# A conv-FFN whose modulation steps, copies and first splits stand in other places

## The chip, the cores and the metric

The kernel runs on one core of a Trainium2 chip. The core has five engines with a queue of instructions each: TensorE (PE in the profile) multiplies matrices and writes its results to PSUM, VectorE (DVE) and ScalarE (ACT) do the element-wise work, GpSimd (POOL) helps them, and SyncE (SP) issues most of the DMA transfers. An engine works through its own queue in program order, and semaphores make one engine wait for another. The metric is the device time of one execution in microseconds (us); the median of several runs counts.

## What is computed

The reference is a transformer of two layers over 1024 rows of 1024 columns and 256 context rows. Layer 0 mixes a gated recurrence with latent attention, layer 1 is a differential attention. Behind each attention stands a conv-FFN, and every normalization is modulated: its shift and scale (and the gates of the branches) are rows of `silu(c) @ w_mod + b_mod`, with `w_mod` of 1024 x 6144 per layer.

```
def conv_ffn(u, w_up, conv_w, conv_b, w_down):
    a, g = jnp.split(u @ w_up, 2, axis=-1)
    g = dwconv(g, conv_w, conv_b, FFN_PAD)
    return (jax.nn.gelu(g) * a) @ w_down
```

`a` and `g` have 2816 columns each, and the convolution runs over three neighbouring rows of the sequence. All is in float32.

## The kernel before

**Products.** A float32 product is made as three TensorE passes (`mm3`, L116 to L118): high times high, high times low, low times high. So each operand is split ahead (`split`): ScalarE casts the high part (L283) and VectorE subtracts it for the low part (L98).

**Up projection** (`up_sequence`). It runs over 22 tiles f of 128 columns of `a` and of `g`. The two halves of the sequence and the two halves of the inner dimension make a 2 x 2 block product, which is done with seven block products in place of eight, by sums of the blocks of the weight (`up_sums`, L997 to L1000) and of the normalized rows (the operands "11", "t1", "t2", "t3", "21", "t4", "22"). Each block product is 12 matmuls of 128x512 into one PSUM bank. Bank B takes four of them in turn: `p1`, then t2 (in `p6`), t3 and t4. Between them its content is copied away by ScalarE: to `p` (`p1_out`, L1062), to the sum `a` and to `g` (both in `take`, L1037). `a`, `g` and `p` have one buffer each. For the tile ahead VectorE convolves `g` (L930 to L932), ScalarE makes the gelu (L933), VectorE multiplies with `a` (L1118), and the result goes to DRAM as `hid`. The body of the loop over f therefore finishes tile f - 1 while it computes tile f. In layer 0 the 256 context rows add two smaller products per tile (`ctx_product`, PSUM tile pC) and an own convolution. The first product of the first tiles may be done in the stage ahead (`self.p1`, L984); in layer 1 these are tiles 0 and 1. The queues hold the instructions in the order in which the code issues them (`manual_schedule`).

**Modulation.** While TensorE works, VectorE makes the products with `w_mod` in chunks of 512 columns (`mod_chunk_dve`): a chunk is a generator of six steps. The first zeroes the accumulator `macc` and loads a 128x1024 piece of `w_mod` into a buffer `mr`, of which there is one; each of the next four accumulates the piece (L194, four instructions for two columns `c` and `c_ctx`, two for one) and loads the next; the last sums over partitions with 4 or 8 small matmuls or two wide ones on TensorE (L204 or L211, PSUM tile `modps`) and copies the result away (L206). `some_mods()` runs one step. Before, each tile of layer 0 has such a place twice behind t1 and once behind `second` (the copy of t3's result), and layer 1 has one each. Nine chunks stand in the up projection of layer 0, three in the down projection of layer 0 and two in the up projection of layer 1.

**Down projection** (`ffn_down`). For rounds of three or four row tiles it runs over the 22 blocks f; each needs a piece of `w_down` and of `hid` (`hr`), loaded and split. **Output projection** (`out_proj`), ahead of the FFN: for each row tile it multiplies, adds the residual, normalizes (`scaled`: a Square on ScalarE at L257 which writes into `xn`, and a product with the row's scale at L260), and turns the rows with transposes on TensorE (`turned`, L270, PSUM tile `ntp`). **Front of layer 1** (`layer1_front`): a list of stages per row tile, each with a lag in steps, set by `staggered`; `scale` makes the row's scale (`rs_t`), `norm` transposes.

Of the kernel before, what the change touches and what calls it, by code (L numbers as in the profile page):

```python
# [18 lines left out]
P = 128  # L19
# [40 lines left out]
class K:  # L60
# [728 lines left out]
    def out_proj(self, l, w_name, tiles, get_yT, begin, units=()):  # L789

        nc, io = self.nc, self.io
        with ExitStack() as st:
            Y = self.sb(st, f"outy{l}", side="right")
            O = self.sb(st, f"out{l}")
            nw = NW - l
            where = [None] * nw + [O] * (KT - nw)
            us = list(units) + [self.unit(io[w_name][k * P:(k + 1) * P, :], pool=where[k], bufs=max(1, where.count(where[k])) if where[k] else 4)
                                for k in range(len(units), KT)]
            gas = {}
            y, h = {}, {}  # L800

            def load(t):
                y[t] = get_yT(Y, t)

            def product(t):
                xt = O.tile([P, D], F32, tag="x", bufs=2, name="x")
                nc.sync.dma_start(xt, (self.h0 if l == 0 else self.h1)(t))
                ps = self.PS.tile([P, 2, 512], F32, tag="p2", bufs=4, name="ops")
                for k in range(KT):
                    for a, n, j in TURNS[t == tiles[0]]:  # L810
                        if k == a and isinstance(y.get(t + n), tuple):
                            made = y[t + n][j]()
                            if j:
                                y[t + n] = made
                    for b in range(2):
                        self.mm3(ps[:, b, :], y[t][k], [x[:, b * 512:(b + 1) * 512] for x in us[k]], k == 0, k == KT - 1)
                h[t] = O.tile([P, D], F32, tag="tmp", bufs=3, name="tmp")
                c = int(t >= NTX)
                if c not in gas:
                    gas[c] = self.ga(O, l, 0, c, "ga")  # L820
                nc.vector.tensor_mul(h[t], ps.rearrange("p a b -> p (a b)"), gas[c])
                (nc.vector if t == tiles[-1] else nc.gpsimd).tensor_tensor(h[t], h[t], xt, op=ADD)
                nc.sync.dma_start(self.hm_d[t], h[t])

            def fill(t):
                if t == tiles[-1]:
                    begin()

            def norm(t):

                xn = O.tile([P, D], F32, tag="xn", bufs=1, name="xn")
                junk = xn.rearrange("p (k c) -> p k c", c=P)
                self.scaled(O, h[t], xn, junk, eng=nc.vector if t == tiles[-1] else None)
                c = slice(t % 4 * P, (t % 4 + 1) * P)
                if t < NTX:
                    self.turned(xn, self.AB2[0], lambda k: self.V[f"{k // 4 + 1}{t // 4 + 1}"][:, k % 4, c])
                    self.column_sums(t)
                else:
                    v = O.tile([P, KT, P], F32, tag="tmp", bufs=3, name="v")
                    self.turned(xn, self.AB2[1], v)  # L840
                    self.split(v, *(x[:, :, (t - NTX) * P:(t - NTX + 1) * P] for x in self.uc))

            self.staggered(tiles, (load, 0), (product, 1 + l), (fill, LAG_N + l), (norm, LAG_N + l))
# [75 lines left out]
    def split_new(self, x, pool=None, tag="w", bufs=4):  # L919

        n = x.shape[-1]
        hi, lo = ((pool or self.W).tile([P, n], F32R, tag=tag + y, bufs=bufs, name="w" + y) for y in "hl")
        self.split(x, hi, lo)
        return hi, lo

# [20 lines left out]
    def ctx_gate(self, F, f, pg):  # L946
        nc = self.nc
        nc.scalar.copy(self.cg[:, 1:1 + CTX], pg)
        gc = F.tile([P, CTX], F32, tag="cgc", bufs=2, name="gc")
        self.convolved(0, f, self.cg, gc, CTX)  # L950
        return gc

# [62 lines left out]
    def up_sequence(self, l, st, F0, chunks):  # L1015
# [25 lines left out]
        def some_mods():  # L1041
            if mods:
                mods.pop(0)()
# [29 lines left out]

        X = banks(0)
        p1(X)
        p1_out(X)
        self.split_columns(U, "t2")
        p6(X)
        self.split_columns(U, "t1")
        product(X["E"], X["s"], 0, "t1", True)  # L1080
# [20 lines left out]
        raws = self.fetch_up(l, 2)  # L1101
        F = self.sb(st, f"later{l}")
        mods += [x for ch in chunks for x in self.mod_steps(F, *ch)]
        per = -(-len(mods) // (NF - 2))
        for f in range(1, NF + 1):
            Y = step.pop(f - 1)
            if f < NF:
# [2 lines left out]
            take(g[:, 1:513], Y["B"], Y["p1"])  # L1110
            gc = F.tile([P, SEQ], F32, tag="gc", name="gc")
            if f < NF:
                X["s"] = self.split_13(X["raw"])
                p1_out(X)
            self.convolved(l, f - 1, g, gc, SEQ)
            product(Y["E"], Y["s4"], 0, "22", False)
            nc.vector.tensor_add(Y["sum"][:, h2], Y["sum"][:, h2], Y["E"])
# [6 lines left out]
            if here:  # L1124
                X["c"] = bank("C")
                self.ctx_product(X["c"][:, :CTX], [X["a21"], [y[:, h2] for y in X["g"]]])
            p6(X)
            product(X["E"], X["s"], 0, "t1", True)
            some_mods()
            if per > 2:  # L1130
                some_mods()
            if here:
                cgc = self.ctx_gate(F, f, X["c"][:, :CTX])
            if f + 1 < NF:
# [13 lines left out]
            if f + 1 < NF:  # L1148
                N["g"] = self.split_new(raws[1])
            product(X["B"], X["g"], 512, "t4", False)  # L1150
            if f + 2 < NF:
                raws = self.fetch_up(l, f + 2)
        while mods:
            some_mods()

    def mod_steps(self, pool, l, ch, nctx):

# [3 lines left out]
    def ffn_down(self, l, rounds, dst, chunks, after):  # L1161

        nc, io = self.nc, self.io
        with ExitStack() as st:
            F = self.sb(st, f"down{l}")
            gas = [self.ga(F, l, 1, c, f"ga{c}") for c in range(2 if l == 0 else 1)]
            extra = []
            if after:
                Un = self.sb(after, "u1cols", side="right")
# [26 lines left out]
                        lambda: self.turned(xn, AB, v), lambda: self.split(v, *u)]  # L1196

            with self.tc.manual_schedule():
                for i in range(3):
                    fetch(i)  # L1200
                split(0)
                for r, tiles in enumerate(rounds):
                    with ExitStack() as s2:
                        PS = self.PS = self.ps(s2, f"psD{l}{r}")
# [5 lines left out]
                        for f in range(NF):  # L1210
                            i = r * NF + f
                            if i + 3 < len(items):
                                fetch(i + 3)
                            if f == 8:
                                for t in tiles:
                                    hts[t] = F.tile([P, D], F32, tag="ht", bufs=8, name="ht")
# [27 lines left out]
    def layer1_front(self):  # L1244

        nc, io = self.nc, self.io
        with ExitStack() as st:
# [4 lines left out]
            with ExitStack() as st2:  # L1252
# [91 lines left out]
                        self.load1(0, "q")  # L1344
                        self.load1(0, "k")
                early = (lambda f: lambda item: f(item[1] + n0) if item[0] == 4 and item[1] + n0 < NT else None)
                self.staggered(items, (early(load), 0), (early(scale), 4), (early(norm), 7), (project, 4), (finish, 5), (first_head, 8))

    def lam_prep(self):

# [219 lines left out]
    def build(self, stop=99):  # L1570
        nc, tc, io = self.nc, self.tc, self.io
        with ExitStack() as st:
# [48 lines left out]
            with ExitStack() as s2:  # L1621
                F0 = self.sb(s2, "begun0")
                self.p1 = {}
                with ExitStack() as s3:
# [3 lines left out]
                    self.ctx_place(F0)  # L1628
                    self.AB2 = [self.mod_finish(0, 1, c) for c in range(2)]
                    self.out_proj(0, "w_out_ab", [*range(NTX, NT), *range(NTX)], self.yT0, lambda: self.begin0(F0))  # L1630
                self.ffn_up(0, F0, [(1, ch, 2) for ch in range(4)] + [(0, ch, 2) for ch in (10, 11)] + [(1, ch, 1) for ch in range(4, 7)])
                self.ctx_columns.close()
            columns = st.enter_context(ExitStack())
            self.ffn_down(0, [range(0, 4), range(4, 7), range(7, NT)], lambda t: self.h1_d[t], range(7, 10), columns)
            with ExitStack() as s2:
                self.PS, self.twos = self.ps(s2, "psL"), 4
                self.lam_prep()
# [70 lines left out]

# [9 lines left out]
```

## Time and profile before

| | us |
|---|---|
| runs | 3426.54, 3425.10, 3422.24 |
| median | 3425.1 |
| profiled execution | 3431.7 |
| its span in the trace | 3429.9 |
| TensorE busy | 3186.3 |
| VectorE busy | 2360.9 |
| ScalarE busy | 1412.1 |
| GpSimd busy | 945.2 |

The span is the time from the first to the last instruction of the profiled execution, which is 1.8 us shorter than its time. Times of rows count from the start of the span. The stages by their rough place: output projection of layer 0 to 877, its up projection to 1505, its down projection to 1845, front of layer 1 to 2185, attention to 2595, output projection to 2735, up projection of layer 1 to 3180, down projection to the end.

### The profile page before, as it was taken

Reading aid. Unit: us, or ns where it says so; the run is one execution under the profiler, and the core shown is the slowest. Engines: PE = TensorE matmul, PEld = TensorE weight load, DVE = VectorE, ACT = ScalarE, POOL = GpSimd, SP = SyncE. Lnnn points to the kernel's source line nnn. Section 1 sums busy time; section 2 is a strip of 40 time slices with the busy share of each in tenths; the row PEclk is TensorE's granted clock in tenths of the full one; section 3 lists DMA queues with packets and bytes.
Section 4 is the critical chain, followed back from the end, with each engine's and each line's share of the span. In section 5 each row is a group of like instructions: output and inputs, shape, how many; then the busy total and the mean of one; then the engine's idle time right before and its main releaser. Section 6 shows DMA issues by size and latency. Waiting matters only on the chain.

```text
span 3429.9 us, 43450 instructions
## 1 busy us (share of the span) xinstructions
PE 3186.3 (93%) x16262; PEld 2633.3 (77%) x16262; DVE 2360.9 (69%) x3381; ACT 1412.1 (41%) x2444; POOL 945.2 (28%) x654
## 2 busy tenths in 40 slices
PE   8998889989799999989899999888888889999998
PEld 4777778878578778868777887777777768888887
DVE  6468978855776777643566687599997687666443
ACT  3355766733422223322243222477763333333322
POOL 2223578864000000000122223277764200000010
PEclk9999999999899999999999999999999999999999
DMA  6224953344122223234755355444414122223553
GB/s 261 70 77 129 285 141 94 89 137 134 47 96 97 97 97 111 97 123 151 249 192 182 120 139 131 146 114 126 111 62 160 62 86 101 90 74 98 181 180 124
DMA packets 232298, 434.07 MB, mean 127 GB/s; under 512 B 21484, under 2 KB 147692, under 8 KB 230296
## 3 DMA queue, kind: packets, MB, share of 16 engines
q1 hardware_dynamic: 230216, 424.49, 39.3%
q10 hardware_dynamic: 1872, 6.82, 0.6%
q8 instruction: 128, 2.10, 0.2%
q14 instruction: 82, 0.67, 0.1%
HBM read 319.89 MB, written 111.34 MB: 126 GB/s over the span
## 4 chain that ended last, share of the span: by engine, by line
PE 54%; DVE 14%; DMA 3%; issue 3%; ACT 3%; POOL 1%; SPq 0%; DVEq 0%; ACTq 0%; POOLq 0%
PE acc L118 4%; PE pB L116 4%; PE pB L118 4%; PE pB L117 4%; PE acc L116 4%; PE acc L117 4%; DVE m L1456 3%; PE pj L116 3%; PE pj L117 3%; PE pj L118 3%; DVE p L1472 3%; PE pE L118 2%; PE pE L116 2%; PE pE L117 2%; PE ops L117 2%
## 5 line engine op out<-in xcount | busy, mean ns | idle before, releaser
L98 DVE TENSOR_TENSOR wl<-wr,wh 128x1024 fp32r<-128x1024 f32 (+2 forms) x285 | 348.8, 1233 | 92.9 <-ACT wh L283 63.4
L116 PE MATMUL acc<-wh,hh 128*128 128x512 f32 x792 | 312.5, 395 | 18.7 <-ACT wh L283 17.1
L118 PE MATMUL acc<-wl,hh 128*128 128x512 f32 x792 | 312.5, 395 | 9.6 <-DVE wl L98 8.9
L117 PE MATMUL acc<-wh,hl 128*128 128x512 f32 x792 | 310.6, 392 | 4.5 <-DVE hl L98 4.5
L1236 POOL TENSOR_TENSOR ht<-ht,dtmp 128x1024 f32<-128x1024 f32 x17 | 45.7, 2715 | 857.1 <-DVE dtmp L1235 857.1
L283 ACT CAST wh<-wr 128x1024 fp32r<-128x1024 f32 (+1 forms) x221 | 220.9, 1008 | 83.4 <-DVE wr L999 72.4
L98 POOL TENSOR_TENSOR wl<-wf,wh 128x1280 fp32r<-128x1280 f32 x64 | 221.9, 3468 | 106.3 <-ACT wh L1491 94.7
L1451 PE MATMUL S<-k,q 128*128 128x512 f32 (+1 forms) x768 | 197.8, 382 | 55.7 <-ACT p L1462 55.5
L116 PE MATMUL pB<-ht,wh 128*128 128x512 f32 x528 | 210.4, 398 | 16.5 <-ACT ht L283 6.5
L98 DVE TENSOR_TENSOR hl<-hr,hh 128x512 fp32r<-128x512 f32 (+1 forms) x110 | 76.0, 691 | 206.7 <-ACT hh L283 206.6
L118 PE MATMUL pB<-lt,wh 128*128 128x512 f32 x528 | 210.3, 398 | 2.2 <-DVE lt L98 2.0
L117 PE MATMUL pB<-ht,wl 128*128 128x512 f32 x528 | 209.5, 397 | 0.8 <-DVE wl L98 0.8
L194 DVE SCALAR_TENSOR_TENSOR macc<-wr,sc,macc 128x512 f32<-128x512 f32 x192 | 135.8, 748 | 105.2 <-DMA wr<-w_mod 104.1
L283 ACT CAST hh<-hr 128x512 fp32r<-128x512 f32 (+1 forms) x110 | 63.7, 579 | 325.0 <-PE acc L118 242.0
L1462 ACT ACTIVATE p<-S,m 128x1280 f32<-128x1280 f32 x128 | 170.8, 1334 | 60.6 <-DVE m L1456 57.5
L1456 DVE TENSOR_REDUCE m<-S 128x1 f32<-128x1280 f32 x128 | 187.1, 1479 | 6.2 <-PE S L1451 5.6
L116 PEld LDWEIGHTS acc<-wh,hh 128*128 128x128 f32 x792 | 149.8, 189 | 53.4 <-ACT wh L283 21.8
L177 POOL MEMSET macc<- 128x512 f32 x24 | 12.4, 526 | 636.8 <-PE modps L211 283.3
L118 PEld LDWEIGHTS acc<-wl,hh 128*128 128x128 f32 x792 | 149.7, 189 | 49.4 <-DVE wl L98 18.6
L1451 PEld LDWEIGHTS S<-k,q 128*128 128x128 f32 x768 | 124.9, 193 | 77.2 <-ACT p L1462 64.5
L116 PE MATMUL pj<-wh,u 128*128 128x512 f32 x448 | 177.6, 396 | 2.5 <-DVE qT L98 2.5
L117 PE MATMUL pj<-wh,u 128*128 128x512 f32 x448 | 178.0, 397 | 0.0
(414 smaller groups left out, 9178.3 us busy)
## 6 DMA issues: line engine op xcount, KB each, us to landing
wr<-ffn_down SPq DMA_DIRECT2D x110, 512.0 KB
wr<-ffn_up SPq DMA_DIRECT2D x90, 512.0 KB
wr<-w_mod SPq DMA_DIRECT2D x76, 512.0 KB
hid<-gc SPq DMA_DIRECT2D x44, 512.0 KB
k<-dk SPq DMA_DIRECT2D x14, 1280.0 KB
hr<-hid SPq DMA_DIRECT2D x66, 256.0 KB
wr<-w_in_c SPq DMA_DIRECT2D x24, 512.0 KB
mr<-w_mod SPq DMA_DIRECT2D x20, 512.0 KB
```

The lines of the kernel that those rows point to most:

```text
L98: e.tensor_tensor(out, x, hi.bitcast(F32), op=SUB)
L116: mm(out, a[0], b[0], start=start, stop=False, skip_group_check=onto)
L117: mm(out, a[1], b[0], start=False, stop=False, skip_group_check=onto)
L118: mm(out, a[0], b[1], start=False, stop=stop, skip_group_check=onto)
L177: nc.gpsimd.memset(acc[c], 0.0)
L194: nc.vector.scalar_tensor_tensor(acc[c], raw[:, kk * 512:(kk + 1) * 512], self.sc[:, 2 * u + kk, c:c + 1], acc[c], op0=MUL, op1=ADD)
L283: self.nc.scalar.copy(hi, x)
L1236: (nc.vector if last else nc.gpsimd).tensor_tensor(hts[t][:, c], hts[t][:, c], tmp[:, c], op=ADD)
L1451: nc.tensor.matmul(Y["S", m][:, c0:c0 + n], heads[h]["q"][m][:, t * P:(t + 1) * P], heads[h]["k"][x, m, j], start=(x == 0), stop=(x == 1))
L1456: nc.vector.tensor_reduce(Y["m", m], Y["S", m][:, :TOK], axis=AX.X, op=ALU.max, negate=True)
L1462: nc.scalar.activation(Y["p", m], Y["S", m][:, :TOK], AF.Exp, bias=Y["m", m], accum_out=Y["s"] if m else s0[:, h, t:t + 1])
L1472: nc.vector.scalar_tensor_tensor(Y["p", 0], Y["p", 1], Y["tt"], Y["p", 0], op0=MUL, op1=ADD)
```

## The change

- In the loop of the up projection the copy of `p` is issued ahead of the split of `s` (`split_13`); at its head, behind the split of t2.
- One modulation step stands in each of four places of a tile: ahead of `p6`, behind t1, behind `second`, behind t4. Three more chunks are made in the up projection of layer 0, and none in its down projection.
- `xn` in `out_proj` has two buffers.
- The first weight and the first `hid` block of the down projection are loaded and split in the last two tiles of the up projection (`fetch_down`, `self.ahead`); the gates' rows (`ga`) are loaded later in `ffn_down`.
- In the front of layer 1 `scale` has lag 5 for 4 and `norm` 8 for 7.
- `cgc` has one buffer, tiles of the splits are 1024 wide whatever is split, and the scratch of the DMA rings is 512.

```diff
             def norm(t):
-                xn = O.tile([P, D], F32, tag="xn", bufs=1, name="xn")
+                xn = O.tile([P, D], F32, tag="xn", bufs=2, name="xn")
...
-        hi, lo = ((pool or self.W).tile([P, n], F32R, tag=tag + y, bufs=bufs, name="w" + y) for y in "hl")
+        hi, lo = ((pool or self.W).tile([P, n if pool else 1024], F32R, tag=tag + y, bufs=bufs, name="w" + y)[:, :n] for y in "hl")
...
-        gc = F.tile([P, CTX], F32, tag="cgc", bufs=2, name="gc")
+        gc = F.tile([P, CTX], F32, tag="cgc", bufs=1, name="gc")
...
         p1(X)
+        self.split_columns(U, "t2")
         p1_out(X)
-        self.split_columns(U, "t2")
         p6(X)
...
-        per = -(-len(mods) // (NF - 2))
         for f in range(1, NF + 1):
...
             if f < NF:
+                p1_out(X)
                 X["s"] = self.split_13(X["raw"])
-                p1_out(X)
             self.convolved(l, f - 1, g, gc, SEQ)
...
+            some_mods()
             p6(X)
             product(X["E"], X["s"], 0, "t1", True)
             some_mods()
-            if per > 2:
-                some_mods()
...
             product(X["B"], X["g"], 512, "t4", False)
+            some_mods()
             if f + 2 < NF:
                 raws = self.fetch_up(l, f + 2)
-        while mods:
-            some_mods()
+            elif f + 2 == NF:
+                raws = self.fetch_down(l)
+            else:
+                self.ahead = self.split_new(raws[1]), self.split_new(raws[0])
...
+    def fetch_down(self, l):
+        w, x = (self.W.tile([P, 1024], F32, tag="wr", bufs=NWR, name="wr") for _ in range(2))
+        self.nc.sync.dma_start(w, self.io["ffn_down"][l, :P, :])
+        self.nc.sync.dma_start(x[:, :512], self.hid_d[0, :, :512])
+        return w, x[:, :512]
...
-                for i in range(3):
+                parts[0] = self.ahead
+                for i in range(1, 3):
                     fetch(i)
-                split(0)
...
+                            if i == 4:
+                                gas = [self.ga(F, l, 1, c, f"ga{c}") for c in range(2 if l == 0 else 1)]
...
-                self.staggered(items, (early(load), 0), (early(scale), 4), (early(norm), 7), (project, 4), (finish, 5), (first_head, 8))
+                self.staggered(items, (early(load), 0), (early(scale), 5), (early(norm), 8), (project, 4), (finish, 5), (first_head, 8))
...
-                self.ffn_up(0, F0, [(1, ch, 2) for ch in range(4)] + [(0, ch, 2) for ch in (10, 11)] + [(1, ch, 1) for ch in range(4, 7)])
+                self.ffn_up(0, F0, [(1, ch, 2) for ch in range(4)] + [(0, ch, 2) for ch in (10, 11)] + [(1, ch, 1) for ch in range(4, 10)])
...
-            self.ffn_down(0, [range(0, 4), range(4, 7), range(7, NT)], lambda t: self.h1_d[t], range(7, 10), columns)
+            self.ffn_down(0, [range(0, 4), range(4, 7), range(7, NT)], lambda t: self.h1_d[t], (), columns)
```

ScalarE in a late tile of layer 1's up projection, before (`s` is the sum of weight blocks that is split for t1 and t3, `wh` the high part; what an instruction waits for stands in brackets):

```order
L1037 COPY g<-pB 128x512 [waits PE_49]
L283 CAST wh<-s 128x1024
L1062 COPY p<-pB 128x512 [waits DVE_49,PE_49,Activation_49]
L933 ACTIVATE gc<-gc 128x1024 [waits DMAHW5_49,DVE_49]
L283 CAST wh<-s 128x512 [waits PE_49,Activation_49]
L1037 COPY a<-pB 128x512 [waits DVE_49,PE_49]
```

The same place after:

```order
L1037 COPY g<-pB 128x512 [waits PE_49]
L1062 COPY p<-pB 128x512 [waits DVE_49,PE_49]
L283 CAST wh<-s 128x1024
L933 ACTIVATE gc<-gc 128x1024 [waits DMAHW3_49,DVE_49]
L283 CAST wh<-s 128x512 [waits PE_49,Activation_49]
L1037 COPY a<-pB 128x512 [waits DVE_49,PE_49]
```

The copy of `p`, which waits for TensorE, has moved from behind the 128x1024 cast to ahead of it; the rest has kept its order.

VectorE in the up projection of layer 0, before, from the sum of weight blocks to the next tile (`modps` holds the sums of a chunk):

```order
L1000 TENSOR_TENSOR s<-wr 128x512
L1071 TENSOR_TENSOR g<-g,pE 128x512
L206 COPY mcol<-modps 128x8
L1145 TENSOR_TENSOR a<-p,pA 128x512
L954 TENSOR_TENSOR gc<-gc,pC 128x256
L98 TENSOR_TENSOR wl<-wr,wh 128x1024
L98 TENSOR_TENSOR wl<-s,wh 128x1024
```

The same engine after, in the third tile of a cycle (L1143 is L1145 of before):

```order
L1000 TENSOR_TENSOR s<-wr 128x512
L1071 TENSOR_TENSOR g<-g,pE 128x512
L194 SCALAR_TENSOR_TENSOR macc<-wr,sc,macc 128x512 x4
L1143 TENSOR_TENSOR a<-p,pA 128x512
L954 TENSOR_TENSOR gc<-gc,pC 128x256
L98 TENSOR_TENSOR wl<-wr,wh 128x1024
L206 COPY mcol<-modps 128x8
L237 SCALAR_TENSOR_TENSOR A<-mcol,cols 128x8 x2
L98 TENSOR_TENSOR wl<-s,wh 128x1024
```

The last accumulation now stands behind t3's copy, and the finish of the chunk behind t4, at the end of the tile.

SyncE between the up and the down projection of layer 0, before (`hr` is a block of `hid`):

```order
L1119 DMA hid<-gc 128x1024
L955 DMA hid<-gc 128x256
L1119 DMA hid<-gc 128x1024
L244 DMA ga<-ga_132 128x1024
L244 DMA ga<-ga_133 128x1024
L1181 DMA hr<-hid 128x512
L1178 DMA wr<-ffn_down 128x1024
```

And after:

```order
L955 DMA hid<-gc 128x256
L1161 DMA wr<-ffn_down 128x1024
L1162 DMA wr<-hid 128x512
L1186 DMA wr<-ffn_down 128x1024
L1118 DMA hid<-gc 128x1024
L955 DMA hid<-gc 128x256
L1118 DMA hid<-gc 128x1024
L1189 DMA hr<-hid 128x512
L1186 DMA wr<-ffn_down 128x1024
```

The first loads of the down projection now stand two stores of `hid` earlier, and the rows of the gates no longer stand ahead of them.

## Rows read from the trace of the kernel before

**Rows 1.** The page, part 1: busy time, share of the span, instructions.

```profile
PE 3186.3 (93%) x16262; PEld 2633.3 (77%) x16262; DVE 2360.9 (69%) x3381; ACT 1412.1 (41%) x2444; POOL 945.2 (28%) x654
```

**Rows 2.** Windows: from:to, length, busy time per engine, granted clock, DMA share, GB/s.

```profile
877.00:1505.00 628.00, 583.25 (x2938) 487.90 (x2936) 436.68 (x588) 185.91 (x277) 7.83 (x15) 0.95 0.27 91
2790.00:3170.00 380.00, 380.00 (x1656) 309.72 (x1655) 268.35 (x308) 131.88 (x176) 0.53 (x1) 1.00 0.27 91
...
2747.00:2765.00 18.00, 14.39 (x58) 10.58 (x58) 17.80 (x19) 5.16 (x6) 0.53 (x1) 1.00 0.00 0
...
1020.00:1026.00 6.00, 6.00 (x33) 6.00 (x34) 4.51 (x8) 2.36 (x4) 1.05 (x2) 0.57 0.01 3
```

**Rows 3.** Timeline of a tile of layer 1's up projection: start, duration, [idle before, releaser].

```profile
2963.66 1.05 ACT L283 CAST wh<-s 128x1024 fp32r<-128x1024 f32 x1
2965.99 0.59 ACT L1062 COPY p<-pB 128x512 f32<-128x512 f32 x1 [1.27 <-issue]
...
2971.78 0.59 ACT L1037 COPY a<-pB 128x512 f32<-128x512 f32 x1 [0.84 <-DVE gc L1118]
...
2964.74 1.23 DVE L98 TENSOR_TENSOR wl<-s,wh 128x1024 fp32r<-128x1024 f32 x1 [2.55 <-ACT wh L283]
...
2970.47 1.22 DVE L1118 TENSOR_TENSOR gc<-gc,a 128x1024 f32<-128x1024 f32 x1 [0.53 <-ACT gc L933]
...
2965.51 0.40 PE L118 MATMUL pB<-l,wh 128*128 128x512 f32 x1
...
2973.96 0.39 PE L116 MATMUL pB<-ht,wh 128*128 128x512 f32 x1
```

**Rows 4.** Waits over the whole span: total us, times, longest.

```profile
DVE macc L194 <- DMA wr<-w_mod: 104.1, 31, 6.8
```

**Rows 5.** Timeline of two tiles of layer 0's up projection, VectorE and TensorE.

```profile
1046.77 2.74 DVE L194 SCALAR_TENSOR_TENSOR macc<-wr,sc,macc 128x512 f32<-128x512 f32 x4 [4.26 <-DMA wr<-w_mod]
1049.42 0.41 DVE L930 TENSOR_SCALAR gc<-cg,cols 128x256 f32<-128x256 f32 x1
...
1057.30 2.74 DVE L194 SCALAR_TENSOR_TENSOR macc<-wr,sc,macc 128x512 f32<-128x512 f32 x4
...
1060.88 1.22 DVE L98 TENSOR_TENSOR wl<-wr,wh 128x1024 fp32r<-128x1024 f32 x1
1062.02 1.22 DVE L98 TENSOR_TENSOR wl<-s,wh 128x1024 fp32r<-128x1024 f32 x1
...
1068.87 0.68 DVE L98 TENSOR_TENSOR wl<-s,wh 128x512 fp32r<-128x512 f32 x1
...
1075.53 2.74 DVE L194 SCALAR_TENSOR_TENSOR macc<-wr,sc,macc 128x512 f32<-128x512 f32 x4 [3.32 <-DMA wr<-w_mod]
...
1019.83 2.63 PE L204 MATMUL modps<-ones,macc 128*128 128x1 f32 x16 [2.54 <-DVE macc L194]
...
1047.09 0.39 PE L116 MATMUL pB<-ht,wh 128*128 128x512 f32 x1
...
1077.70 2.43 PE L204 MATMUL modps<-ones,macc 128*128 128x1 f32 x16 [2.71 <-issue]
```

**Rows 6.** Timeline of ScalarE at the last row tile of both output projections.

```profile
869.55 1.06 ACT L257 ACTIVATE xn<-tmp 128x1024 f32<-128x1024 f32 x1 [6.28 <-PE ntp L270]
...
2727.22 1.06 ACT L257 ACTIVATE xn<-tmp 128x1024 f32<-128x1024 f32 x1 [6.28 <-PE ntp L270]
```

**Rows 7.** Timeline of TensorE in both down projections, matmuls with idle time ahead.

```profile
1505.92 0.80 PE L116 MATMUL acc<-wh,hh 128*128 128x512 f32 x1 [13.16 <-ACT wh L283]
...
1644.74 0.50 PE L116 MATMUL acc<-wh,hh 128*128 128x512 f32 x1 [1.73 <-ACT wh L283]
...
1688.57 0.50 PE L118 MATMUL acc<-wl,hh 128*128 128x512 f32 x1 [0.63 <-DVE wl L98]
...
3179.15 0.50 PE L118 MATMUL acc<-wl,hh 128*128 128x512 f32 x1 [1.29 <-DVE wl L98]
```

**Rows 8.** Timeline of TensorE in the front of layer 1.

```profile
1867.10 1.68 PE L270 MATMUL ntp<-ident,x 128*128 128x128 f32 x8 [4.31 <-DVE rs_t L130]
```

More of the change, by code (lines that the diff above doesn't have):

```diff
@@ L1150, in up_sequence @@
             product(X["B"], X["g"], 512, "t4", False)
+            some_mods()
             if f + 2 < NF:
                 raws = self.fetch_up(l, f + 2)
-        while mods:
-            some_mods()
+            elif f + 2 == NF:
+                raws = self.fetch_down(l)
+            else:
+                self.ahead = self.split_new(raws[1]), self.split_new(raws[0])
+        assert not mods
+    def fetch_down(self, l):
[3 more added lines that the diff above has]
+        return w, x[:, :512]
     def mod_steps(self, pool, l, ch, nctx):
@@ L1165, in ffn_down @@
             F = self.sb(st, f"down{l}")
-            gas = [self.ga(F, l, 1, c, f"ga{c}") for c in range(2 if l == 0 else 1)]
             extra = []
@@ L1710 @@
     arrays = layout({k: np.asarray(v) for k, v in inputs.items()})
-    nc = bacc.Bacc("TRN2", target_bir_lowering=False, num_devices=1, dynamic_dma_scratch_size=1024)
+    nc = bacc.Bacc("TRN2", target_bir_lowering=False, num_devices=1, dynamic_dma_scratch_size=512)
     io = {k: nc.dram_tensor(k, v.shape, F32, kind="ExternalInput").ap() for k, v in arrays.items()}
```

## Prediction, on record before the changed kernel was run

> **What bounds the kernel now.** I read the engine totals first: TensorE is busy for 93% of the span [rows 1], so time is won or lost only where TensorE stands still or runs at its lower clock. Next the windows by stage. In the up projection of layer 1, TensorE is busy for all of a 380 us stretch at a granted clock of 1.00; in that of layer 0 it is busy for 583 of 628 us at 0.95 [rows 2]. So the first has nothing to gain and can only lose; the second loses about 45 us to idle time, plus some to the clock. Then TensorE's timeline, for the rows with idle time in brackets; the terms below are those.
>
> The clock must be priced first. After the 2.54 us wait at 1019.83 [rows 5] the next 6 us ran at 0.57 of 2.4 GHz, mostly the 1.2 GHz level, which costs 6 x 0.43 = 2.6 us. The 18 us from 2747 hold two waits of 1.45 us and stayed at 1.00 [rows 2]. So I charge 2.6 us behind a wait of 2.5 us or more, and nothing behind one of 1.5 us or less.
>
> **Loss 1: the copy of p ahead of the cast (layer 1's up projection).** TensorE makes seven products in a tile: p1 on bank B, "22" on E, t2 on B, t1 on E, t3 on B, "21" on A, t4 on B. Before, ScalarE copies g (end of t4), casts s, and only then copies p. The cast starts at 2963.66 and the copy of p at 2965.99, just behind the last matmul of p1, which starts at 2965.51 [rows 3]. Now the copy of p stands ahead of the cast, so the cast waits for p1. The copy lasts 0.59, and a row on ScalarE starts 0.1 us before the one ahead ends, so the cast starts at 2965.99 + 0.48 = 2966.47, which is 2.81 us later. Behind the cast stand, one for one, the subtraction on VectorE (2964.74), the convolution, the gelu, the product with the other half (2970.47, 1.22) and the copy of a (2971.78, 0.59), since a has one buffer. Nothing in that chain has a pause to give back but the 0.5 us for the gelu, which is part of it. So the copy of a ends at 2972.37 + 2.81 = 2975.18; t3 needs it, because it overwrites bank B. t3 started at 2973.96, so TensorE waits 2975.18 + 0.05 - 2973.96 = 1.27 us, in each tile that copies p. Tiles 0 and 1 have their first product from the stage before, so 20 copy p; 18 of these have no modulation step: 18 x 1.27 = 22.9 us. No clock loss by the price above.
>
> In layer 0 a context product of 2.8 us stands between "22" and t2, so a shift of 2.81 is just covered there in tiles without steps; its VectorE nevertheless starts 2.81 later.
>
> **Loss 2: where the modulation steps stand.** A chunk has six steps: a load, four accumulations (each frees the buffer and issues the next load), and a finish with small TensorE matmuls, which cannot run before the last accumulation. Four steps per tile make a cycle of three tiles with two chunks: A (load, u0, u1, u2), B (u3, finish, load, u0), C (u1, u2, u3, finish). Slots 1 and 2 have nothing of VectorE between them, so u1 and u2 of C are still a pair, and the second waits for its load: 3.32 us of idle time [rows 5]. Such waits sum to 104 us before [rows 4]. With u2 in slot 4, A has 3.3 us of it as well.
>
> I add up VectorE's chain from T, the end of t4 (1033.2 in the tile shown). From the subtraction of s to that of s4 takes 1062.02 to 1069.5, 7.45 us; from the end of an accumulation to the next one's place behind t3, 1049.4 to 1057.3, 7.9; from there to the end of the split of g, 1060.0 to 1062.0, 2.0; an accumulation for two columns takes 2.7. TensorE reaches t3 at T + 13.9 and needs 25.0 for an undisturbed tile [rows 5].
> - A: the subtraction of s starts at T + 4.55 (T + 1.75 before, as in [rows 3], and 2.81 of shift), s4 is done at 12.0, and u0 starts 4.3 later as in the trace, ending at 19.0; u1 ends at 29.6, g's split at 31.6; u2's load lands 3.3 after u1, and u2 ends at 35.6.
> - B starts at T + 25. VectorE is free only at 35.6 (not at 29.55): s4 ends at 43.05, u3 at 45.75. The finish may start 0.6 before that, as at 1077.70 [rows 5]; its place is 25 + 13.9 = 38.9. Wait 6.3, finish 2.4: B takes 33.7.
> - C: s4 at 12.0, u1 14.7, u2 20.7, u3 31.3. The finish stands behind t4 at 25.0: wait 5.7, finish 2.4: C takes 33.1.
>
> Together 91.8 us for two chunks. Before, a chunk for two columns took 1077.70 - 1019.83 = 57.87 with its two tiles. For a chunk with one column (accumulations of 1.5, finish 1.05) the same sum gives waits of 1.8 and 2.7 and about 81 us per cycle. Over the 18 tiles: before 6 x 57.9 + 6 x 25.0 + 3 = 500; after 3 x 91.8 + 6 x 2.6 of clock + 3 x 81 = 534. I take +34. Ends: +15 if the clock holds and the loads come a little sooner, +47 if the small waits cost clock too.
>
> In layer 1's up projection the same pattern runs once, with 12 steps in tiles 1 to 3: waits of about 4 in B, and 4 besides the 1.27 in C, with clock 5; so 22.9 + 4 + 5.3 + 5 = 37, less some in A, which has no p copy: +35 (+25 to +40).
>
> **Gains.** (a) A second xn: the Square of the last tile waited 6.28 us for the transposes of the tile ahead, in both output projections [rows 6]. Behind it the splits of t2 now stand ahead of other head work, so I keep 11 of 12.6 (6 to 12.6). (b) The down projection of layer 0 began with a wait of 13.16; its first split is now made earlier. The hidden block 1 still follows the last store of the up projection, so some 2 to 3 us of waiting stay, but the clock is kept: -13 (10 to 16). In layer 1: -1.3 [rows 7]. (c) Three chunks leave the down projection: its six waits from 1644.74 to 1688.57 sum to 7.75 [rows 7]; with 2.6 of clock and some of three finishes of 1: -11 (3 to 13; the low end if the waits were for the transfers). (d) One step more lag in layer 1's front: the 4.31 wait goes, and about 2 of clock behind it (2.6 by the price above, as a bound): -6.3 [rows 8] (0 to 6.9: nothing if rs_t is late anyway). Sum: -43 (-20 to -48). The single cgc buffer, narrower tiles and DMA scratch I cost at nothing: the context's convolution is far ahead of its next use; were cgc late, 22 tiles x 0.3 would be 7.
>
> **Sum.** -43 + 34 + 35 = +26 on the profiled 3431.7, which lies 6.6 above the median of the runs shown. So 3425.1 + 26 = 3451; I say 3450.
>
> **A rule weighed.** The rows say that waits of 1.3 to 1.5 us leave the clock at 1.00 [rows 2]. The Trainium skill ("TensorE: Matmul & The Clock Gate", "A second HAM failure mode: psum-queue depth-cycling") says that an engine which pauses often between groups of matmuls, as it cycles through PSUM banks, can swing between both levels. It speaks against a pause in each tile at bank B. By it the forecast would be that of rival 3; the trace before shows such pauses only two or three in a row.
>
> **The rivals.**
> 1. Faster: the delay on ScalarE doesn't reach TensorE. This turns on one number, the 1.6 us between the end of the copy of a (2972.37) and t3 (2973.96) [rows 3]: if the cast shifts by less, up1 costs nothing and up0's chains start earlier. Then -43 + about 10 for the adjacent steps: 3392. Against it: the copy of p already starts at the end of p1 in the trace, so it cannot come sooner. Chance 0.12.
> 2. No change: loss 1 holds, but the steps of layer 0 fit (their loads are issued earlier and land before VectorE gets there): -43 + 35 + 5: 3422. For it: half of TensorE's waits here come from one load per chunk. Against: C's pair is still a pair. Chance 0.12.
> 3. Much slower: every 1.3 us pause costs clock as the larger do: 18 x 2.6 = 47 more: 3497. Chance 0.06.
>
> The forecast has 0.70, with its own range of 3430 to 3475. That the steps taken out of the down projection change nothing (its waits were for transfers) would add 8 inside it. The range 3412 to 3480 leaves out most of rival 1 and rival 3. Two runs of this kernel differ by up to 0.13%, so 0.2%, 7 us, tells apart: faster 0.15, same 0.12, slower 0.73.
>
> **What the profile after would show.** In layer 1's up projection: copies of p directly behind those of g, casts 2.8 us later, and a TensorE wait of about 1.3 on "ACT a" at t3 in each tile, clock 1.00; TensorE busy for about 355 of 380 us. In layer 0: waits of 5 to 6 us ahead of the small matmuls, twice in three tiles, and behind t4 as well as t1. No 13 us wait at the down projection, none near its 130th us, and no 4.31 in the front. If the pauses at t3 are absent, loss 1 was wrong and with it the sign; if they stand at 1.3 and the time still falls, loss 2 was oversized.

## The result, and the profile after

The changed kernel takes 3470.7 us (median of 4 runs, 3465.6 to 3472.2) against 3424.6 for the kernel before in the same series: a ratio of 1.0132 (95% interval 1.0115 to 1.0150), so 46 us slower. The forecast was 3450 with a range of 3412 to 3480. The profiled execution took 3469.4 us, 37.7 more than that of before; the other 8 us of the medians are the spread of single runs, since the profiled run of before lay 7 above its median and this one 1 below.

The first table says where the 37.7 us arose. Each stage runs from its first matmul on TensorE's timeline to the first one of the next, the last one to its last matmul. Rows that no edit touches (the first, attention) still differ by up to 3 us.

| stage | before | after | difference |
|---|---|---|---|
| ahead of output projection 0 | 736.9 | 734.0 | -2.9 |
| output projection 0 | 150.5 | 145.2 | -5.2 |
| up projection 0, with the wait at its end | 618.6 | 647.7 | +29.1 |
| down projection 0 and front of layer 1 | 679.4 | 664.7 | -14.7 |
| attention 1 | 421.4 | 420.6 | -0.8 |
| output projection 1 | 133.5 | 129.2 | -4.3 |
| up projection 1 | 437.1 | 474.4 | +37.3 |
| down projection 1 | 243.1 | 242.2 | -0.9 |

The end wait of 13.16 us in the third row of before [rows 7] is gone after. Booked to the down projection behind it, it means that the up projection of layer 0 itself lost 42 us and that the down projection and the front won 28. The windows of the changed kernel (from:to, length, busy time of PE, PEld, DVE, ACT and POOL, granted clock, DMA share, GB/s) show both up projections; the rows of before are [rows 2].

```profile
900.00:1520.00 620.00, 572.06 (x2831) 473.34 (x2831) 430.52 (x583) 170.97 (x255) 9.40 (x18) 0.94 0.28 98
...
2850.00:3200.00 350.00, 331.99 (x1429) 266.56 (x1428) 223.91 (x256) 116.98 (x153) 0.00 (x0) 1.00 0.24 78
```

In layer 1 TensorE was busy for all of its window before; now it idles for 18 of 350 us, at a granted clock of 1.00. Why, stands in the timeline of one tile, ScalarE, VectorE and TensorE one after the other, which answers to [rows 3].

```profile
2966.06 0.59 ACT L1037 COPY g<-pB 128x512 f32<-128x512 f32 x1 [3.39 <-PE pB L118]
2968.83 0.59 ACT L1062 COPY p<-pB 128x512 f32<-128x512 f32 x1 [2.17 <-PE pB L118]
2969.31 1.05 ACT L283 CAST wh<-s 128x1024 fp32r<-128x1024 f32 x1
2975.02 1.06 ACT L933 ACTIVATE gc<-gc 128x1024 f32<-128x1024 f32 x1 [4.65 <-DVE gc L932]
...
2977.43 0.59 ACT L1037 COPY a<-pB 128x512 f32<-128x512 f32 x1 [0.84 <-DVE gc L1117]
...
2970.39 1.23 DVE L98 TENSOR_TENSOR wl<-s,wh 128x1024 fp32r<-128x1024 f32 x1 [5.31 <-ACT wh L283]
...
2976.11 1.23 DVE L1117 TENSOR_TENSOR gc<-gc,a 128x1024 f32<-128x1024 f32 x1 [0.53 <-ACT gc L933]
...
2978.06 0.50 PE L116 MATMUL pB<-ht,wh 128*128 128x512 f32 x1 [1.06 <-ACT a L1037]
...
2998.66 0.50 PE L116 MATMUL pB<-ht,wh 128*128 128x512 f32 x1 [1.06 <-ACT a L1037]
```

The reader is to follow the copy of p, which waits 2.17 us for TensorE; the cast right behind it; VectorE, idle for 5.31 us where it was 2.55; and at the end t3, which waits for the copy of a. Its pause of 1.06 us recurs in every tile, and t3 to t3 takes 20.60 us, where it took 19.23 before, from 2973.96 [rows 3] to this row:

```profile
2993.19 0.39 PE L116 MATMUL pB<-ht,wh 128*128 128x512 f32 x1
```

In layer 0 the finishes of the chunks wait, as TensorE's timeline shows (compare 2.54 and 2.71 in [rows 5]; rows of x13 and x3 are cut off by the end of their view, in full they are x16 with 3.54 us and x4 with 3.57 us).

```profile
1048.07 2.90 PE L204 MATMUL modps<-ones,macc 128*128 128x1 f32 x13 [5.52 <-issue]
...
1089.33 0.50 PE L116 MATMUL pB<-ht,wh 128*128 128x512 f32 x1 [2.26 <-ACT g L1037]
...
1095.47 2.33 PE L204 MATMUL modps<-ones,macc 128*128 128x1 f32 x16 [1.54 <-issue]
...
1145.52 2.72 PE L211 MATMUL modps<-macc,ones 128*1 128x512 f32 x3 [5.54 <-issue]
...
1234.89 1.02 PE L211 MATMUL modps<-macc,ones 128*1 128x512 f32 x2 [2.00 <-DVE macc L194]
...
1319.64 1.05 PE L204 MATMUL modps<-ones,macc 128*128 128x1 f32 x8 [1.85 <-DVE macc L194]
...
1359.33 1.62 PE L204 MATMUL modps<-ones,macc 128*128 128x1 f32 x8 [2.51 <-DVE macc L194]
```

A cycle of three tiles with two chunks for two columns runs from 1048.07 to 1145.52, 97.5 us. The wait of 2.26 at t4 was not forecast. ScalarE and VectorE around it show its source:

```profile
1086.91 0.42 ACT L933 ACTIVATE gc<-gc 128x256 f32<-128x256 f32 x1 [9.80 <-DVE gc L932]
1087.24 1.55 ACT L283 CAST wh<-wr 128x1024 fp32r<-128x1024 f32 x2
1088.69 0.58 ACT L1037 COPY g<-pB 128x512 f32<-128x512 f32 x1
...
1082.77 2.74 DVE L194 SCALAR_TENSOR_TENSOR macc<-wr,sc,macc 128x512 f32<-128x512 f32 x4 [3.35 <-DMA wr<-w_mod]
1085.43 0.41 DVE L930 TENSOR_SCALAR gc<-cg,cols 128x256 f32<-128x256 f32 x1
```

The second of a pair of accumulations waits 3.35 us for its load. Behind it on VectorE stands the context's convolution, behind that on ScalarE the context's gelu, and behind the gelu in ScalarE's queue the copy of g, which frees bank B for t4. The last matmul of t3 starts at 1081.16, so by these rows ScalarE, idle for 9.8 us, could have made the copy some 7 us earlier, had it stood ahead of the gelu; no run tried that.

The gains came. The Square of the last row tile waits for its own data and no longer for the transposes [rows 6], and the down projection begins at 1526.90 without the wait of 13.16 [rows 7]. Its second block, 9 us later, still waits 3.69 us:

```profile
860.18 1.06 ACT L257 ACTIVATE xn<-tmp 128x1024 f32<-128x1024 f32 x1 [0.57 <-DVE tmp L822]
```

```profile
1536.21 0.50 PE L116 MATMUL acc<-wh,hh 128*128 128x512 f32 x1 [3.69 <-ACT wh L283]
```

### The profile page after: what moved, and what is told of

Same layout as the page of the kernel before. It is cut to its first block, busy times and chain, and to the rows that moved or that the text cites. A ratio compares the mean times of both kernels' runs of the same rounds, so it can differ in the third digit from the quotient of the medians.

```text
span 3467.6 us, 43472 instructions
## 1 busy us (share of the span) xinstructions
PE 3202.6 (92%) x16262; PEld 2635.2 (76%) x16262; DVE 2362.5 (68%) x3381; ACT 1414.0 (41%) x2444; POOL 944.8 (27%) x654
## 4 chain that ended last, share of the span: by engine, by line
PE 45%; DVE 18%; issue 6%; ACT 6%; DMA 2%; POOL 1%; SPq 0%; DVEq 0%; ACTq 0%; POOLq 0%
PE acc L118 4%; PE acc L116 4%; PE acc L117 4%; PE pB L116 3%; PE pB L118 3%; PE pB L117 3%; PE pj L116 3%; PE pj L117 3%; PE pj L118 3%; DVE p L1482 2%; DVE wl L98 2%; DVE m L1466 2%; PE ops L117 2%; PE ops L116 2%; PE ops L118 2%
## 5 line engine op out<-in xcount | busy, mean ns | idle before, releaser
L118 PE MATMUL acc<-wl,hh 128*128 128x512 f32 x776 | 305.3, 393 | 8.4 <-DVE wl L98 5.5
L116 PE MATMUL acc<-wh,hh 128*128 128x512 f32 x776 | 305.2, 393 | 5.6 <-ACT wh L283 5.6
L117 PE MATMUL acc<-wh,hl 128*128 128x512 f32 x776 | 303.5, 391 | 0.0
L116 PE MATMUL pB<-ht,wh 128*128 128x512 f32 x528 | 219.3, 415 | 46.0 <-ACT a L1037 22.9
L933 ACT ACTIVATE gc<-gc 128x256 f32<-128x256 f32 (+1 forms) x66 | 55.9, 848 | 344.7 <-DVE gc L932 344.7
L98 DVE TENSOR_TENSOR wl<-s,wh 128x1024 fp32r<-128x1024 f32 x88 | 84.0, 955 | 161.2 <-ACT wh L283 161.2
L116 PE MATMUL pj<-wh,u 128*128 128x512 f32 x448 | 176.9, 395 | 2.5 <-DVE qT L98 2.5
```

The costliest lines, as they stand in the source:

```text
L98: e.tensor_tensor(out, x, hi.bitcast(F32), op=SUB)
L116: mm(out, a[0], b[0], start=start, stop=False, skip_group_check=onto)
L117: mm(out, a[1], b[0], start=False, stop=False, skip_group_check=onto)
L118: mm(out, a[0], b[1], start=False, stop=stop, skip_group_check=onto)
L933: nc.scalar.activation(gc, gc, AF.Gelu_apprx_tanh)
```

## The experiments

Medians are in us, ratios are against the kernel before on the same chip, with 95% intervals. None of these kernels leaves out any of the computation.

### Undo the order of p

```diff
             if f < NF:
-                p1_out(X)
                 X["s"] = self.split_13(X["raw"])
+                p1_out(X)
```

> The changed kernel with one edit undone: in the loop the copy of p stands behind the split of s again. Theory (the late cast drives the chain cast, subtraction, convolution, product, copy of a, t3): the pauses of 1.06 us at t3 vanish from layer 1's up projection and its tile goes back from 20.6 to 19.2 us, 18 x 1.37 = 25 us; in layer 0 VectorE starts 2.8 us earlier, so each of the two finishes of a cycle waits about 2.8 less, 6 x 5.6 = 34 us at most. Together 50 to 60 us less than 3471, so 3410 to 3420, which is below the kernel before. Rival (the order on ScalarE is harmless, and the modulation steps alone make the loss): 3465 to 3475, pauses at t3 still there.

Measured: 3393.4, ratio 0.9912 (0.9896 to 0.9929). One pair of lines turns the change from 46 us slower into 31 us faster. The pauses in layer 1 are gone:

```profile
2800.00:3140.00 340.00, 340.00 (x1487) 278.83 (x1487) 231.24 (x262) 119.98 (x160) 0.00 (x0) 1.00 0.26 85
```

and layer 0's finishes wait about what they did before the change (the row of x15 is cut off by the end of its view, in full it is x16 with 3.40 us):

```profile
1040.06 1.92 PE L204 MATMUL modps<-ones,macc 128*128 128x1 f32 x16 [2.78 <-issue]
...
1082.98 3.19 PE L204 MATMUL modps<-ones,macc 128*128 128x1 f32 x15 [3.12 <-issue]
```

The rival (steps alone) is out. The gain is larger than expected, 77 for 50 to 60. The waits of t4 for the copy of g are gone too, and no wait stands ahead of the finishes of the one-column chunks any more; neither was in the expectation.

### The order of p alone, on the kernel before

```diff
             if f < NF:
-                X["s"] = self.split_13(X["raw"])
                 p1_out(X)
+                X["s"] = self.split_13(X["raw"])
```

> The kernel before with one edit of the change alone: the copy of p ahead of the split of s. Theory: +25 us in layer 1's up projection (18 to 20 tiles of 1.37) and, in layer 0, the finish of each of six two-column chunks waits 2.8 us longer, +17; together 3460 to 3470. Rival (the order is harmless): 3425. If only layer 1 reacts: 3450.

Measured: 3482.2, ratio 1.0166 (1.0151 to 1.0181): 57 us, more than the whole change. Up projection 1 takes 464.4 us for 437.1, up projection 0 644.6 for 618.6. TensorE's rows show both places:

```profile
1086.88 3.44 PE L204 MATMUL modps<-ones,macc 128*128 128x1 f32 x16 [4.97 <-issue]
...
2968.99 0.50 PE L116 MATMUL pB<-ht,wh 128*128 128x512 f32 x1 [1.06 <-ACT a L1037]
```

With the steps in their old places the finish waits 5.0 for 2.7, the 2.3 us that the later cast leaves of its 2.8. The rest of the 26 us in that stage (17 expected) is seen in the rows too: the one-column chunks, which waited for nothing before, now wait 1.5 to 1.7, and the finish itself takes 3.44 us for 2.43 [rows 5], with a granted clock of 0.51 in the 6 us from 1086.90.

### The steps back, and both back

The steps return to their old places and three chunks to the down projection; in the second kernel p is behind the split as well.

```diff
+        per = -(-len(mods) // (NF - 2))
         for f in range(1, NF + 1):
...
-            some_mods()
             p6(X)
             product(X["E"], X["s"], 0, "t1", True)
             some_mods()
+            if per > 2:
+                some_mods()
...
             product(X["B"], X["g"], 512, "t4", False)
-            some_mods()
...
-                self.ffn_up(0, F0, [(1, ch, 2) for ch in range(4)] + [(0, ch, 2) for ch in (10, 11)] + [(1, ch, 1) for ch in range(4, 10)])
+                self.ffn_up(0, F0, [(1, ch, 2) for ch in range(4)] + [(0, ch, 2) for ch in (10, 11)] + [(1, ch, 1) for ch in range(4, 7)])
...
-            self.ffn_down(0, [range(0, 4), range(4, 7), range(7, NT)], lambda t: self.h1_d[t], (), columns)
+            self.ffn_down(0, [range(0, 4), range(4, 7), range(7, NT)], lambda t: self.h1_d[t], range(7, 10), columns)
```

> The changed kernel with its modulation steps in their old places and three chunks in the down projection again; p still ahead. Theory: up0 falls from 42 us above the kernel before to about 17 above, up1 loses some 10 us of its two tiles with steps, the down projection gets 5 to 10 us back; 3440 to 3455, the pauses at t3 in layer 1 stay at 1.06. Rival (the four places are harmless, all of the loss comes from the copy of p): 3470 to 3480, since the chunks in the down projection cost.

> The changed kernel with both undone: p behind the split, steps and chunks as before. What is left of the change are the second xn, the earlier first splits of the down projection and the lags of the front. Theory: these bring 9 + 12 + 6 = 27 us; 3395 to 3402. Rival (they bring nothing at the end, since the time saved is given back by the next wait): 3420 to 3427.

Measured: 3448.7, ratio 1.0066 (1.0051 to 1.0081), and 3399.0, ratio 0.9922 (0.9907 to 0.9937). Both are in their ranges, and the pauses of t3 in the first stay at 1.06 as expected. With the first experiment and the changed kernel they make a square:

| | old places | four places |
|---|---|---|
| p behind the split | 3399.0 | 3393.4 |
| p ahead | 3448.7 | 3470.7 |

p ahead costs 50 us with the old places and 77 with the four. The four places lose 22 us with p ahead; with p behind they come out 5.6 lower, which the intervals of the two ratios, that overlap, don't separate from nothing. So the places alone are no loss: by the stages they cost 3 us in up projection 0 for three more chunks and 9 in up projection 1, and give back 15 in the down projection. What the prediction priced as the loss of the places is an interaction: VectorE, started 2.8 us late, comes too late with the accumulations that the finishes need. It is not full, since it is busy for 430.5 of the 620 us in the window above; it waits, and the experiments with the pieces of w_mod price its waits for loads.

The upper left kernel also prices the rest of the change. By the stages of its profiled execution the output projections take 4.6 and 4.9 us less, and up projection 0 to attention 19.4 less together; by the medians it is 26 in all. It keeps the single cgc buffer, the changed tiles of the splits and the smaller DMA scratch, which no run undoes one by one, so they are not where the loss comes from.

### Two buffers for the sum tile

```diff
-            X["sum"] = B.tile([P, SEQ], F32, tag="a", name="a")
+            X["sum"] = B.tile([P, SEQ], F32, tag="a", bufs=2, name="a")
```

> The changed kernel with two buffers of the sum tile a, the order of the copies unchanged. Theory (t3 waits through the copy of a, which waits for the product on VectorE that reads the old a): the copy of a now waits only for its place in ScalarE's queue behind the gelu and the cast of s4, which end at about 2973.7 against 2974.5 for the product (layer 1's timeline shifted by 2.81), so the pause at t3 falls from 1.06 to 0.1 to 0.4 us, 15 to 20 us less in layer 1's up projection; layer 0 hardly moves, since its waits go through the accumulations: 3450 to 3460. Rival (the pause comes from something else behind the late cast, such as the split of s itself or bank B): 3470, pauses at 1.06.

Measured: 3450.9, ratio 1.0075 (1.0058 to 1.0091). The order of the copies is that of the change, the cast is as late, yet the copy of a now stands right behind the cast of s4 and waits for nothing, and TensorE's window is full again but for 2 us:

```profile
2970.86 0.60 ACT L283 CAST wh<-s 128x512 fp32r<-128x512 f32 x1
2971.36 0.58 ACT L1037 COPY a<-pB 128x512 f32<-128x512 f32 x1
```

```profile
2850.00:3190.00 340.00, 337.90 (x1454) 271.26 (x1454) 228.48 (x260) 117.07 (x156) 0.00 (x0) 1.00 0.25 81
```

Up projection 1 falls from 474.4 to 456.7. A tile takes 19.63 us from t3 to t3 (2952.36 to 2971.99), so 0.4 of the 1.37 us stays, within the 0.1 to 0.4 expected. This shows the last link of the chain, the copy of a waiting for the product that reads the old a. Up projection 0 stays at 647.5, so its loss takes another way; the rows there name the accumulations (macc) and the copy of g.

### Two buffers for the pieces of w_mod

```diff
-            raw = (pool.tile([P, 1024], F32, tag="mr", bufs=1, name="wr") if fine else
+            raw = (pool.tile([P, 1024], F32, tag="mr", bufs=2, name="wr") if fine else
```

Three kernels carry this edit: with p behind and four places, with p behind and old places, and on the changed kernel as it is.

> The changed kernel with p behind the split of s (as the first experiment, 3393) and two buffers for the pieces of w_mod, so that a piece is loaded while the one ahead is accumulated. Theory (the finishes wait because the second of two adjacent accumulations waits 3.3 us for its load): the waits of 2.4 to 3.1 ahead of the small matmuls in layer 0 and of 1.0 and 2.2 in layer 1 nearly vanish, with the clock behind them; 6 x 5 + 5 = 25 to 35 us less: 3358 to 3368. Rival (VectorE is simply full there, and the loads only fill idle time that the next wait would take): 3388 to 3395.

> The changed kernel with p behind the split, steps and chunks in their old places (as the fourth experiment, 3399), and two buffers for the pieces of w_mod. Theory: its five regular finish waits of 2.7 with their clock go, 6 x 5 = 30 less, while the three chunks in the down projection stay: 3368 to 3378; the four places with two buffers should be ahead by the 10 us of the down projection. Rival: 3395 to 3400.

> The changed kernel (p ahead of the split, four places) with two buffers for the pieces of w_mod and nothing else. Theory (both losses add up on VectorE: the late start of its work, and the waits for loads): without the load waits the finish in the second tile of a cycle waits 2 to 3 us for 5.5, that behind t4 nearly nothing, and the waits of 2.2 for the copy of g go; the pauses of 1.06 in layer 1 stay. 25 to 35 us less: 3436 to 3446. Rival (the late start alone makes the waits): above 3462.

Measured: 3379.1, ratio 0.9868 (0.9854 to 0.9883); 3374.3, ratio 0.9853 (0.9838 to 0.9867); 3451.0, ratio 1.0077 (1.0062 to 1.0092). So the second buffer is worth 14, 25 and 20 us. The second kernel is as expected; the first gains half of what was expected and the third two thirds, and both lie between the theory and its rival. That the four places would be ahead of the old ones by 10 us was wrong: they come out 5 us behind, which the intervals don't separate from nothing. In the third kernel the wait in the second tile of a cycle fell to 4.0 only, and the one behind t4 rose from 1.5 to 3.1, where nearly nothing was expected. Waits remain; first with p behind, then with p ahead. That they remain because the finish stands directly behind the accumulation that it needs is tested next, for p behind alone.

```profile
1037.03 1.92 PE L204 MATMUL modps<-ones,macc 128*128 128x1 f32 x16 [1.31 <-issue]
```

```profile
1087.36 2.98 PE L204 MATMUL modps<-ones,macc 128*128 128x1 f32 x16 [3.10 <-issue]
```

### An empty step ahead of each finish

```diff
-        return [lambda: next(it, None)] * 6
+        return [lambda: next(it, None)] * 5 + [lambda: None, lambda: next(it, None)]
```

Both with p behind and two buffers; the first with four places, the second with the old ones.

> As the sixth experiment (p behind the split, four places, two buffers for the pieces of w_mod: 3379), with one empty step ahead of each chunk's finish, so that the small matmuls stand one place behind the last accumulation; 84 steps then fill the 84 places of 21 tiles. Theory (the finishes still wait 1.0 to 1.6 us because they stand directly behind the accumulation that they need): the waits ahead of the small matmuls go, 6 x 1.2 plus some in the one-column chunks and layer 1; 3362 to 3372. Rival (VectorE's work is the limit, and another wait takes their place): 3376 to 3382.

> As the seventh experiment (p behind the split, old places, two buffers: 3374), with the empty step ahead of each finish; 63 steps fill 63 places of 21 tiles, three chunks stay in the down projection. Theory: five waits of about 1.0 and one of 3.1 go: 3366 to 3371, and the four places with the empty step come out 0 to 8 below this one, since they spare the down projection its chunks. Rival: 3372 to 3377.

Measured: 3363.5, ratio 0.9823 (0.9808 to 0.9838), and 3362.6, ratio 0.9818 (0.9802 to 0.9835). No wait ahead of the small matmuls is left in either, and layer 0's up projection runs like layer 1's. With p behind, then, the order made the waits that were left. First the one with four places, then the one with the old:

```profile
960.00:1460.00 500.00, 500.00 (x2655) 422.69 (x2654) 385.90 (x531) 152.49 (x229) 7.36 (x14) 1.00 0.32 113
2790.00:3110.00 320.00, 320.00 (x1400) 262.48 (x1399) 217.59 (x248) 114.05 (x152) 0.00 (x0) 1.00 0.25 83
```

```profile
960.00:1450.00 490.00, 490.00 (x2598) 413.91 (x2597) 366.65 (x498) 149.34 (x226) 6.83 (x13) 1.00 0.29 102
```

These are the fastest kernels here, some 61 us below the kernel before. The second is faster than the 3366 to 3371 expected. The four places, expected 0 to 8 us ahead, are not, and the intervals do not separate the two: they win in the down projection and the front about what they cost in the up projections (574.0 against 568.7 in that of layer 0, 665.5 against 675.1 behind it, 439.4 against 436.4 in layer 1).

### The lags of layer 1's front alone

```diff
-                self.staggered(items, (early(load), 0), (early(scale), 4), (early(norm), 7), (project, 4), (finish, 5), (first_head, 8))
+                self.staggered(items, (early(load), 0), (early(scale), 5), (early(norm), 8), (project, 4), (finish, 5), (first_head, 8))
```

> The kernel before with the lags of the front of layer 1 alone. Theory: the 4.31 us wait goes with some clock, -6: 3418 to 3421. Rival (the row's scale is late by as much in the new place): 3424 to 3427.

Measured on the kernel before: 3416.7 over 10 runs, ratio 0.9978 (0.9968 to 0.9987), 8 us, a little more than expected. The first eight transposes of the front start without a wait and take 1.03 us together, for the 1.68 of [rows 8]:

```profile
1860.05 1.03 PE L270 MATMUL ntp<-ident,x 128*128 128x128 f32 x8
```

## Why the prediction was right, and where it was off

**As a whole.** Forecast were 26 us more on the profiled execution; it took 37.7 more. Loss 2 measured 8 above its term, loss 1 measured 2 above and the gains 5 below, and the stages that no edit touches gave back 4. The medians differ by 8 us more than the profiled executions, so the 46 us lie 20 above the forecast, inside its range.

**Loss 1, right.** The copy of p delays the cast, the product, the copy of a and t3, each link as forecast; two buffers for a cut the last link, and all but 0.4 us of the delay went. The forecast of 1.27 us per tile measured 1.37 from t3 to t3. Up projection 1 lost 37 us for the 35 forecast.

**Loss 2, near in size but filed under the wrong name.** Forecast were waits of 6.3 and 5.7 in a cycle, and 1.8 and 2.7 with one column; the rows show 5.5, and 2.3 + 1.5 in two parts, then 1.9 and 2.5. A cycle of 91.8 and two times 2.6 of clock should take 97.0; it took 97.5. That it agrees so well is in part luck: the waits sum to 9.3 us for 12.0, and the clock, below, took the difference. The up projection lost 42 for 34, most of the rest in the one-column cycles (1319.64 less 1234.89, 84.8 us for 81). Each of them holds one wait of 2.5 us (2.7 forecast), which the prediction's own price charges with 2.6 us and its sum did not. But the sum took the start of VectorE at T + 4.55, with the shift of the cast already in it, and booked the result as the cost of the places. The square of experiments shows that the places cost nothing without that shift. Only rival 1 let both losses hang on the shift. A reader who went by the two terms would have undone the places as well, and with the places alone undone 50 us of the loss stay.

**Small steps that were wrong.** That in tiles without steps layer 0 covers the shift held for TensorE: with the order of p alone it waits for nothing in the last tiles. But the accumulations that fit before no longer did, one-column ones too, as the order of p alone showed with 26 us in that stage. The wait of t4 for the copy of g was not on the list. I looked for what each late instruction delays on VectorE, not for what stands behind the context's gelu on ScalarE. The 0.3 us per tile, at which a late cgc was priced, stands in no row.

**Gains, nearly right as a sum.** Forecast 43; the stages show -5.2 and -4.3 (11 forecast), -27.8 from the end of up projection 0 to attention (30) and -0.9 (1.3): 38. Within the 27.8 two terms make up for each other: the first splits bring about 9 us for the 13 forecast, since with the chunks in their old places the wait of 13.16 went but the down projection itself took 3.8 longer, and the chunks that left it bring 12 to 15 for 11 (estimates across runs). The upper end of the forecast's range, 48, is 50 by its own terms.

**The clock, half right.** The price was 2.6 us behind waits of 2.5 us or more and nothing behind 1.5 or less. In layer 1 the second half held: 17 pauses of 1.06 us in 350 us left the granted clock at 1.00. In layer 0 it was too low. The windows behind the waits of the cycle, and behind a finish with one column, show it:

```profile
1048.00:1056.00 8.00, 7.93 (x27) 7.01 (x28) 3.49 (x7) 1.87 (x3) 1.05 (x2) 0.51 0.20 68
1090.00:1102.00 12.00, 10.46 (x37) 8.42 (x36) 8.35 (x16) 1.64 (x2) 1.05 (x2) 0.64 0.30 98
1359.00:1366.00 7.00, 6.67 (x20) 5.59 (x21) 2.58 (x6) 0.00 (x0) 0.53 (x1) 0.55 0.51 169
```

Behind the wait of 5.52 the lower level of 1.2 GHz cost about 8 x 0.49 = 3.9 us. Behind the waits of 2.26 and 1.54, for which the price has no figure, it cost about 12 x 0.36 = 4.3 us. That is 8.2 us in a cycle for the 5.2 forecast. The Trainium skill ("TensorE: Matmul & The Clock Gate", "A second HAM failure mode: psum-queue depth-cycling") reports a kernel in which frequent short pauses between groups of matmuls made the clock swing. The pauses of 1.06 us, one in each tile of 20.60 us, show nothing of it, and rival 3 falls with them.

**The rivals.** Rival 1 was the right picture of another kernel: with p behind, 3393.4 against the 3392 worked out for it. Rival 2 (the steps fit in layer 0) is refuted by the waits of 5.5.

## What to carry to other kernels

A queue in program order makes the position of one waiting instruction a start time for everything behind it: before an eviction is moved ahead of other work, look up when its input is ready, and which chain begins behind it. Where two edits act on the same engine, price each with the other undone; a chain that is added up with one edit inside it cannot say which edit to take back. A total that agrees is no proof of its terms: look at the waits and the clock one by one. A result that is needed by the engine that bounds the kernel should be asked for one place later than it is made: the empty step was worth 16 us with the four places and 12 with the old ones.

## What was unexpected of the hardware

A pause costs more than its idle time says. t3 waited 1.06 us by its row, but the tile grew by 1.37. The rows of the changed kernel around the pause show two parts of the difference:

```profile
2976.39 0.39 PE L117 MATMUL pE<-ht,wl 128*128 128x512 f32 x1
2976.62 0.39 PE L118 MATMUL pE<-lt,wh 128*128 128x512 f32 x1
2978.06 0.50 PE L116 MATMUL pB<-ht,wh 128*128 128x512 f32 x1 [1.06 <-ACT a L1037]
2978.40 0.39 PE L117 MATMUL pB<-ht,wl 128*128 128x512 f32 x1
```

The matmul ahead of the pause is shown with 0.39 us, though the next one starts 0.23 after it when nothing is in the way, and the first one behind the pause takes 0.50 and 0.34 us to the next start. So the start-to-start time of a repeated row is the better measure of a short wait.
